# A squared-ReLU MLP in split fp32: the first product by Strassen's seven products, the second as a phase of its own

## The chip, the cores and the metric

The kernel runs on one core of a Trainium2 chip. The metric is the device time of one launch, in microseconds. The core has a matrix engine (TensorE, PE in the profile, with its weight loads shown as PEld), a vector engine (VectorE, DVE), an activation engine (ScalarE, ACT), a general engine (GpSimd, POOL), and a queue engine (SyncE, SP), which here issues every load and store. SBUF is the on-chip memory, PSUM the eight banks of 128 x 512 fp32 into which TensorE accumulates, DRAM the memory outside.

## What is computed

One inference step of a diffusion backbone with one layer, on 128 context tokens and 2048 latent tokens: 17 tiles of 128 tokens. Tile 0 is the context, with modulation vectors of its own; tiles 1 to 16 are latent. The model width D is 1024, the MLP's inner width DFF 4096.

```python
def block(x, s0, mod, ...):
    sh1, sc1, ga1, sh2, sc2, ga2 = mod
    h = rmsnorm(x, norm_mix_l) * (1.0 + sc1) + sh1
    o, s_new = mixer(h, s0, ...)     # projections, chunked DeltaNet scans, spatial gating, output projection
    x = x + ga1 * o
    h = rmsnorm(x, norm_ffn_l) * (1.0 + sc2) + sh2
    x = x + ga2 * (jnp.square(jax.nn.relu(h @ w_ff1_l)) @ w_ff2_l)
    return x, s_new
```

A last rmsnorm (`norm_final`) follows for both streams. The change is in the MLP line alone: `h @ w_ff1` is 2176 x 1024 by 1024 x 4096, and the second product 2176 x 4096 by 4096 x 1024.

## The kernel before

**Split products.** Every large product is taken on operands split in two: `H` is the value rounded to the type fp32r (an ACT copy), `L` the rest (a DVE subtraction), each of the same size as the value. `mm3` (L205 to L210) issues three matmuls for each pair: H by H, H by L, L by H. In a matmul the first operand (128 x 128) is loaded into the array, the second streams past it, up to 512 columns at a time. `load_split` (L176 to L185) loads a 128 x 512 block of weights from DRAM and splits it.

**Order of the work.** The program is written as lists of small steps that are merged (`interleave`, and a list of events with due times for the scan phase, whose bounds stand in `WINDOWS`). A planner with a simulated timeline then fixes each engine's order. Every engine works in its own fixed order and waits on semaphores for what it needs; loads and stores go in order through SP.

**Phases.** Modulation vectors (`mod_steps`: w_mod in blocks of 128 x 512, multiplied on DVE, added up on PE), input projection and convolution, forward scan over the tiles, backward scan. In the backward scan (events from `NT` on) each tile also gets its gates and the output projection (`o_steps`; matmuls named pj, with operands oH and oL), which writes the residual to `x2_d` in DRAM. `h2_steps` then takes a tile of `x2_d`, normalises it, transposes it in eight 128 x 128 pieces on PE, applies scale and shift on ACT, and stores the MLP's input, transposed, to `h2_d`: per tile two loads and two stores of 256 KB. The tiles go from 16 down to 0; `h2_steps` runs inside the scan phase for tiles 16 to 13 (`GROUPS[0]`) and inside the MLP for the 13 others.

**The MLP** (L1311 to L1492) handles four groups of tiles: (16..13), (12..9), (8..5) and (4..0). For each group it goes through eight blocks of 512 columns of DFF. `wload` brings 8 blocks of w_ff1 and 8 of w_ff2 of 256 KB (L183, L184 split them); the pools `wp` (48 buffers) and `stage` that hold them are the same as in the phases before. `ff1` makes 4 products of 128 columns of DFF by the group's tokens: 8 x 3 matmuls of 512 columns into one bank (named f), or, for the last group with its 640 tokens, 2 x 8 x 3 of 320 columns. Then ReLU on ACT (L1443), the square on DVE (L1444), and the split into zH (L1445, ACT) and zL (L1446, DVE), which stay in SBUF. The second product (`part`, matmuls named yps or pm) takes for each tile and each half of D the four blocks j, 4 x 3 matmuls, into one bank, and DVE adds the bank to a sum in SBUF (L1470; ACT copies it for the first block). After a group's last block `finish` multiplies by the gate, adds `x2_d`, normalises and stores; for the last group `residual` and `close` do this with most of it ahead of the last block. The last 16 steps of `mod_steps` (jc 10 and 11) run inside the first group. `split_h` loads the next group's `h2_d` and splits it (L1334). No barrier stands between the scan phase and the MLP: both use the pools `wp`, `stage` and `pmp`.

Of the kernel before, what the change touches and what calls it, by code (L numbers as in the profile page):

```python
# [17 lines left out]
P = 128  # L18
D = 1024
# [9 lines left out]
GROUPS = [(16, 15, 14, 13), (12, 11, 10, 9), (8, 7, 6, 5), (4, 3, 2, 1, 0)]  # L29
# [23 lines left out]
NV = 7  # L53
WINDOWS = [2.46, 0.03, -0.51, 1.06, -1.61, 18.16, 17.58, 18.3,
# [4 lines left out]
def hybrid_step(  # L59
# [42 lines left out]
    x2_d = dp.tile([NTOK, D], F32, name="x2_d")  # L102

# [54 lines left out]
    pmp = ctx.enter_context(tc.tile_pool(name="pmp", bufs=1, space=PSUM))  # L158
# [10 lines left out]
    wp = ctx.enter_context(tc.tile_pool(name="wp", bufs=48))  # L169
    sp = ctx.enter_context(tc.tile_pool(name="stage", bufs=NS))  # L170
# [34 lines left out]
    def mm3(ps, trip, first=True, last=True):  # L205
        n = len(trip)
        for i, (lh, ll, rh, rl) in enumerate(trip):
            T.matmul(ps, lh, rh, start=first and i == 0, stop=False)  # L208
            T.matmul(ps, lh, rl, start=False, stop=False)  # L209
            T.matmul(ps, ll, rh, start=False, stop=last and i == n - 1)  # L210
# [6 lines left out]
    def mod_steps(jc, pool):  # L217
# [3 lines left out]
        def f(k):  # L221
            raw = raw_w(w_mod[0, k * P : (k + 1) * P, jc * 512 : (jc + 1) * 512], sp, "raw")
# [8 lines left out]
            if k == KT - 1:  # L231
                ps = pm1()
# [550 lines left out]
    def h2_steps(t, psum, tmp):  # L783
# [4 lines left out]
        def norm2():  # L788
            u["x"] = x = [w512("x"), w512("x")]
# [31 lines left out]
    with ExitStack() as ph:  # L821
# [432 lines left out]
        for i, u in enumerate(units):  # L1254
# [9 lines left out]
            if i >= NT:  # L1264
# [4 lines left out]
                if u["t"] in GROUPS[0]:  # L1269
# [39 lines left out]


    with ExitStack() as ph:  # L1311
        p4h = ph.enter_context(tc.tile_pool(name="p4h", bufs=1))
        p4 = ph.enter_context(tc.tile_pool(name="p4", bufs=1))
        psy = ph.enter_context(tc.tile_pool(name="p4y", bufs=3, space=PSUM))
        psf = ph.enter_context(tc.tile_pool(name="p4f", bufs=3, space=PSUM))

        late_mods = [st for jc in range(10, 12) for st in mod_steps(jc, p4)]
        ga2 = []
        nf = [wrow(norm_final[n * 512 : n * 512 + 512].unsqueeze(0)) for n in range(2)]

        def split_h(gi):

            tiles = GROUPS[gi]
            c0, n = tiles[-1] * P, len(tiles) * P
            hH, hL, steps = [], [], []

            def f(k, s, m):
                if s == 0:
                    hH.append(p4h.tile([P, 640], F32R, tag=f"hH{k}", name="hH4"))
                    hL.append(p4h.tile([P, 640], F32R, tag=f"hL{k}", name="hL4"))  # L1330
                raw = w512("hraw")
                load(out=raw[:, :m], in_=h2_d[:, k, c0 + s : c0 + s + m])
                A.copy(hH[k][:, s : s + m], raw[:, :m])
                V.tensor_tensor(out=hL[k][:, s : s + m], in0=raw[:, :m], in1=f32(hH[k])[:, s : s + m],  # L1334
                                op=ALU.subtract)

            for k in range(KT):
                for s, m in segments(n):
                    steps.append(lambda k=k, s=s, m=m: f(k, s, m))
            return hH, hL, steps  # L1340

        def segments(n):
            return [(0, 512)] if n == 512 else [(0, 320), (320, 320)]

        def wload(b, steps=[]):
            w1 = []
            for k in range(KT):
                w1.append(load_split(w_ff1[0, k * P : (k + 1) * P, b * 512 : (b + 1) * 512]))
                for st in steps[k : k + 1]:
                    st()  # L1350
            w2 = [[load_split(w_ff2[0, (b * 4 + j) * P : (b * 4 + j + 1) * P, m * 512 : (m + 1) * 512])
                   for j in range(4)] for m in range(2)]
            return w1, w2

        NB = DFF // 512
        ny = []
        finishing = []
        nxt = split_h(0)
        for gi, tiles in enumerate(GROUPS):
            if gi == 1:  # L1360
                ga2 += [wrow(mod_d[1:2, 5 * D + n * 512 : 5 * D + n * 512 + 512]) for n in range(2)]
            nt = len(tiles)
            segs = segments(nt * P)
            hH, hL, _ = nxt
            y = [p4.tile([P, D], F32, tag=f"y{i}", name="y4") for i in range(nt)]
            pos = {t: (t - tiles[-1]) * P for t in tiles}

            def finish(i, t, y=y):
                yt = y[i]
                for n in range(2):  # L1370
                    ga = ga2[n]
                    if cond(t) == 0:
                        ga = wrow(mod_d[0:1, 5 * D + n * 512 : 5 * D + n * 512 + 512])
                    sl = slice(n * 512, (n + 1) * 512)
                    x = w512("x4")
                    load(out=x, in_=x2_d[t * P : (t + 1) * P, sl])
                    V.tensor_tensor(out=yt[:, sl], in0=yt[:, sl], in1=ga, op=ALU.mult)
                    V.tensor_tensor(out=yt[:, sl], in0=yt[:, sl], in1=x, op=ALU.add)
                ss = smp.tile([P, 1], F32, tag="ss", name="ss")
                r = smp.tile([P, 1], F32, tag="r", name="r")  # L1380
                junk = p4.tile([P, D], BF16, tag="junk", name="junk")
                A.activation(junk, yt, AF.Square, accum_out=ss)
                rsqrt_cols(r, ss, 1, 1.0 / D, EPS)
                for n in range(2):
                    sl = slice(n * 512, (n + 1) * 512)
                    V.scalar_tensor_tensor(out=yt[:, sl], in0=yt[:, sl], scalar=r, in1=nf[n], op0=ALU.mult,
                                           op1=ALU.mult)
                store(out=yrow(t), in_=yt)

            gates, sums, outs = {}, {}, {}  # L1390

            def residual(i, t, y=y, gates=gates):

                for n in range(2):
                    ga = ga2[n]
                    if cond(t) == 0:
                        ga = wrow(mod_d[0:1, 5 * D + n * 512 : 5 * D + n * 512 + 512])
                    sl = slice(n * 512, (n + 1) * 512)
                    x = w512("x4")
                    load(out=x, in_=x2_d[t * P : (t + 1) * P, sl])  # L1400
                    V.tensor_tensor(out=y[i][:, sl], in0=y[i][:, sl], in1=ga, op=ALU.mult)
# [135 lines left out]
```

## Time and profile before

| | us |
|---|---|
| median of 3 runs | 2792.97 |
| lowest, highest | 2790.7, 2798.1 |
| the profiled execution | 2793.13 |
| its span, from first to last activity | 2791.4 |

The profile is one execution recorded by the hardware. Busy time is the time in which an engine had an instruction at work. A row of the timeline gives the start, the length, the engine, the line of the program, the operation, what it writes and reads, the shape, and how many records it joins; in brackets what the engine waited for. Matmuls are pipelined: the length of one is its latency, and the distance between two starts is what it costs. A row of a table of groups gives the line, engine, operation, names, shape and count, then the busy time and the mean length in ns, then the idle time before them and what ended it. A row of stretches gives start and end, length, and for PE, PEld, DVE, ACT and POOL the busy time and number of records, then the clock granted to TensorE as a share of full speed, the busy share of the DMA engines, and GB/s. A plain fp32 matmul appears as two records, a split (fp32r) one as one.

### The profile page before, as it was taken

Reading aid. Unit: us, or ns where it says so; the run is one execution under the profiler, and the core shown is the slowest. Engines: PE = TensorE matmul, PEld = TensorE weight load, DVE = VectorE, ACT = ScalarE, POOL = GpSimd, SP = SyncE. Lnnn points to the kernel's source line nnn. Section 1 sums busy time; section 2 is a strip of 40 time slices with the busy share of each in tenths; the row PEclk is TensorE's granted clock in tenths of the full one; section 3 lists DMA queues with packets and bytes.
Section 4 is the critical chain, followed back from the end, with each engine's and each line's share of the span. In section 5 each row is a group of like instructions: output and inputs, shape, how many; then the busy total and the mean of one; then the engine's idle time right before and its main releaser. Section 6 shows DMA issues by size and latency. Waiting matters only on the chain.

```text
span 2791.4 us, 45476 instructions
## 1 busy us (share of the span) xinstructions
PE 2742.4 (98%) x16466; PEld 2326.1 (83%) x16466; DVE 1722.4 (62%) x3688; ACT 1284.3 (46%) x3137; POOL 225.9 (8%) x448
## 2 busy tenths in 40 slices
PE   8999998999999899999999999999999999999998
PEld 5999997888887777888878888888888888899988
DVE  5867656777777887865556574454744556444456
ACT  4655555555555566544334343343433434422332
POOL 3121113111111111100000000000000000000000
PEclk9999998999999999999999999999999999999999
DMA  8866648555455666535244443344433454322232
GB/s 292 270 199 209 197 140 279 169 162 160 153 165 184 210 215 220 182 123 161 87 136 151 140 155 99 110 133 133 152 107 96 131 153 141 120 71 61 72 95 83
DMA packets 339910, 426.74 MB, mean 153 GB/s; under 512 B 27404, under 2 KB 187580, under 8 KB 339686
## 3 DMA queue, kind: packets, MB, share of 16 engines
q1 hardware_dynamic: 339686, 423.85, 48.5%
q8 instruction: 129, 2.11, 0.3%
q14 instruction: 95, 0.78, 0.1%
HBM read 338.38 MB, written 85.37 MB: 152 GB/s over the span
## 4 chain that ended last, share of the span: by engine, by line
PE 86%; DMA 7%; DVE 4%; ACT 1%; issue 1%; SPq 1%; POOL 0%; POOLq 0%; ACTq 0%; DVEq 0%
PE f L208 8%; PE f L209 8%; PE f L210 8%; PE yps L210 7%; PE yps L208 7%; PE yps L209 7%; PE pj L208 6%; PE pj L210 6%; PE pj L209 6%; PE pm L208 3%; PE pm L210 3%; PE pm L209 3%; PE pd L867 3%; DMA raw<-in_w_ff_dram 2%; DMA qT<-qT_d 1%; DMA raw<-in_w_mod_dram 1%
## 5 line engine op out<-in xcount | busy, mean ns | idle before, releaser
L184 DVE TENSOR_TENSOR wL<-raw,wH 128x512 fp32r<-128x512 f32 x584 | 393.3, 690 | 200.4 <-ACT wH L183 192.8
L183 ACT CAST wH<-raw 128x512 fp32r<-128x512 f32 x584 | 354.6, 622 | 334.1 <-DMA raw<-in_w_ff_dram 269.9
L208 PE MATMUL f<-hH,wH 128*128 128x512 f32 (+1 forms) x1280 | 457.1, 358 | 1.8 <-ACT rl L1443 1.8
L209 PE MATMUL f<-hL,wH 128*128 128x512 f32 (+1 forms) x1280 | 454.7, 357 | 0.0
L210 PE MATMUL f<-hH,wL 128*128 128x512 f32 (+1 forms) x1280 | 451.7, 357 | 0.0
L208 PE MATMUL yps<-wH,zH 128*128 128x512 f32 x816 | 318.9, 391 | 0.0
L209 PE MATMUL yps<-wL,zH 128*128 128x512 f32 x816 | 317.7, 389 | 0.0
L210 PE MATMUL yps<-wH,zL 128*128 128x512 f32 x816 | 313.7, 389 | 0.0
L208 PEld LDWEIGHTS f<-hH,wH 128*128 128x128 f32 x1280 | 240.2, 188 | 33.8 <-ACT rl L1443 3.6
L209 PEld LDWEIGHTS f<-hL,wH 128*128 128x128 f32 x1280 | 240.3, 188 | 30.1
L210 PEld LDWEIGHTS f<-hH,wL 128*128 128x128 f32 x1280 | 240.2, 188 | 30.0
L1444 DVE TENSOR_TENSOR sq<-rl 128x512 f32<-128x512 f32 (+1 forms) x160 | 96.4, 609 | 263.8 <-ACT rl L1443 263.8
L1443 ACT ACTIVATE rl<-f 128x512 f32<-128x512 f32 (+1 forms) x160 | 83.7, 532 | 318.1 <-PE f L210 318.1
L208 PE MATMUL pj<-kH,wH 128*128 128x386 f32 (+2 forms) x568 | 190.5, 338 | 0.3 <-DVE kH L450 0.3
L210 PE MATMUL pj<-kH,wL 128*128 128x386 f32 (+2 forms) x568 | 190.3, 335 | 0.0
L209 PE MATMUL pj<-kL,wH 128*128 128x386 f32 (+2 forms) x568 | 189.5, 334 | 0.0
L1470 DVE TENSOR_TENSOR y<-y,yps 128x512 f32<-128x512 f32 x171 | 114.0, 683 | 109.2 <-PE yps L210 109.1
L208 PEld LDWEIGHTS yps<-wH,zH 128*128 128x128 f32 x816 | 153.2, 188 | 32.9 <-issue 0.9
L210 PEld LDWEIGHTS yps<-wH,zL 128*128 128x128 f32 x816 | 153.1, 188 | 32.8 <-issue 0.9
L209 PEld LDWEIGHTS yps<-wL,zH 128*128 128x128 f32 x816 | 153.2, 188 | 31.1
L167 POOL TENSOR_TENSOR r<-rsq,nhalf 128x1 f32<-128x1 f32 (+1 forms) x38 | 22.3, 588 | 1589.4 <-DVE rsq L166 1589.4
L1446 DVE TENSOR_TENSOR zL<-sq,zH 128x512 fp32r<-128x512 f32 (+1 forms) x160 | 96.5, 611 | 68.6 <-ACT zH L1445 67.4
(354 smaller groups left out, 5583.9 us busy)
## 6 DMA issues: line engine op xcount, KB each, us to landing
raw<-in_w_ff_dram SPq DMA_DIRECT2D x512, 256.0 KB
raw<-in_w_mod_dram SPq DMA_DIRECT2D x96, 256.0 KB
x<-x_d SPq DMA_DIRECT2D x68, 256.0 KB
raw<-in_w_in_dram SPq DMA_DIRECT2D x48, 256.0 KB
hH<-hH_d SPq DMA_DIRECT2D x42, 256.0 KB
hL<-hL_d SPq DMA_DIRECT2D x42, 256.0 KB
gb<-g_d SPq DMA_DIRECT2D x34, 256.0 KB
KK<-kk_d SPq DMA_DIRECT2D x34, 256.0 KB
```

The costliest lines, as they stand in the source:

```text
L167: G.tensor_tensor(out=out, in0=t[:np_, :n], in1=nhalf[:np_, :n], op=ALU.pow)
L183: A.copy(h, raw)
L184: V.tensor_tensor(out=lo, in0=raw, in1=f32(h), op=ALU.subtract)
L208: T.matmul(ps, lh, rh, start=first and i == 0, stop=False)
L209: T.matmul(ps, lh, rl, start=False, stop=False)
L210: T.matmul(ps, ll, rh, start=False, stop=last and i == n - 1)
L867: T.matmul(p[:, h, :], lhs[:, h, :], rhs[:, h, :], start=True, stop=True)
L1443: A.activation(rl[:, :m], ps[:, :m], AF.Relu)
L1444: V.tensor_tensor(out=sq[:, :m], in0=rl[:, :m], in1=rl[:, :m], op=ALU.mult)
L1446: V.tensor_tensor(out=zl[:, s : s + m], in0=sq[:, :m], in1=f32(zh)[:, s : s + m], op=ALU.subtract)
L1470: V.tensor_tensor(out=ys, in0=ys, in1=ps, op=ALU.add)
```

## The change

- **First product by Strassen's method.** The pools `wp`, `stage` and `pmp` are closed (`wst.close()`) after the scan phase, and new pools are opened. 2048 latent tokens are taken in two groups of 1024 (tiles 9 to 16, then 1 to 8). Tokens (two halves of 512), D (two halves of 512) and pairs of 128 columns of DFF form a 2 x 2 by 2 x 2 block product. In the form used (Winograd's), seven products of sums of blocks take the place of eight. `token_steps` makes the token operands of a group once: 28 loads of 256 KB from `h2_d`, 16 DVE sums, 28 splits (copy on ACT, subtraction on DVE), kept in seven buffers `hop`. `weight_steps` makes the weight operands of one unit (256 columns of DFF): two loads of 512 KB, four sums, seven splits (eight in the second group). `unit` takes the seven products, each 4 x 3 matmuls of 512 columns, partly on top of one another in PSUM (`onto`), adds the rest on DVE, applies ReLU and square, and stores four blocks of 256 KB to a new DRAM buffer `z_d`. There are 2 x 16 units; the weights of a unit are prepared among the steps of the unit before it.
- **Tile 0** doesn't fit the block form. `single` computes it in the second group: 48 matmuls of 128 columns for each unit.
- **h2.** `h2_steps` now runs in the scan phase for tiles 16 to 9; the nine others run two steps at a time inside the first units.
- **The second product is a phase of its own,** with new pools. Tiles go in six groups, (14..16), (11..13), (8..10), (5..7), (2..4), (0, 1). For each group all 32 blocks j of DFF are added up in PSUM (`part`), two banks a tile. For each pair of blocks `operands` loads w_ff2 (two loads of 512 KB) and z (one load) and splits them. w_ff2 is thus read six times instead of four, and z is written to DRAM and read back. `finish` reads the banks directly. The steps of `mod_steps` for jc 10 and 11 move into the first group of this phase.
- The launch also sets a size for a DMA scratch area (`dynamic_dma_scratch_size=1024`).

```diff
+    z_d = dp.tile([P, DFF // P, NTOK], F32, name="z_d")
...
-                if u["t"] in GROUPS[0]:
+                if u["t"] > 8:
                     spread(i + p3[8], i + p3[9], h2_steps(u["t"], pj, fraw), "fill")
...
+    wst.close()
...
+        def token_steps(c0):
+            ops, b, tt = {}, {}, {}
+            def raw(n, kp):
+                kh, th = divmod(n, 2)
+                r = t512("hraw")
+                load(out=r, in_=h2_d[:, kh * 4 + kp, c0 + th * 512 : c0 + th * 512 + 512])
+                return r
+            def put(i, kp, src):
+                if kp == 0:
+                    ops[i] = fh.tile([P, 4, 2, 512], F32R, tag="hop", name="hop", bufs=7)
+                A.copy(ops[i][:, kp, 0, :], src)
+                V.tensor_tensor(out=ops[i][:, kp, 1, :], in0=src, in1=f32(ops[i])[:, kp, 0, :], op=ALU.subtract)
+            def p1(kp):
+                put(1, kp, raw(0, kp))
+            def p5(kp):
+                x, y = raw(1, kp), raw(0, kp)
+                V.tensor_tensor(out=x, in0=x, in1=y, op=ALU.subtract)
+                tt[kp] = x
+                put(5, kp, x)
...
+            return ops, [lambda f=f, kp=kp: f(kp) for f in (p1, p5, p6, p7, p2) for kp in range(4)]
...
+        def weight_steps(jp, extra):
...
+                    load(out=t, in_=w_ff1[0, kh * 512 : kh * 512 + 512, jp * 256 : jp * 256 + 256]
+                         .rearrange("(a p) c -> p a c", p=P))
...
+        def unit(jp, c0, w, ops):
+            def product(i, onto=None):
+                if onto is None:
+                    ps[i] = bank()
+                p = ps[i if onto is None else onto]
+                h, lo = w[i]
+                mm3(p, [(h[:, kp, :], lo[:, kp, :], ops[i][:, kp, 0, :], ops[i][:, kp, 1, :]) for kp in range(4)],
+                    first=onto is None, more=onto is not None)
...
+            def s7():
+                product(7)
+                p7 = t512("p7")
+                A.copy(p7, ps[7])
+                V.tensor_tensor(out=p7, in0=p7, in1=u["x"], op=ALU.add)
+                V.tensor_tensor(out=p7, in0=p7, in1=u["p5"], op=ALU.add)
+                rl2(p7, p7)
+                out(1, 1, p7)
...
+            return [s1, s5, s6, s7, s3, s2, s4]
+
+        def single(jp, w, x):
+            ps = bank()
+            for i, (a, b) in enumerate(((1, 2), (0, 4))):
+                mm3(ps[:, i * P : i * P + P],
+                    [(w[n][0][:, kp, :], w[n][1][:, kp, :], x[0][:, kh * 4 + kp, :], x[1][:, kh * 4 + kp, :])
+                     for kh, n in enumerate((a, b)) for kp in range(4)])
...
+        later = [st for t in range(8, -1, -1) for st in h2_steps(t, bank, t512, t512)]
+        ops, steps = token_steps(9 * P)
+        w, prep = weight_steps(0, False)
+        interleave(steps, prep)
+        for n, (gi, jp) in enumerate(todo):
+            main = unit(jp, c0, w, ops)
+            if gi == 1:
+                main.append(lambda jp=jp, w=w: single(jp, w, x0))
+            nw, prep = weight_steps(todo[n + 1][1], todo[n + 1][0] == 1) if n + 1 < len(todo) else (None, [])
+            extra = later[:2]
+            del later[:2]
...
+            interleave(*[x for x in (main, prep, extra) if x])
+            if n == NP - 1:
+                ops, steps = token_steps(P)
+                for st in steps:
                     st()
...
+        def weights(j):
+            raw = gw.tile([P, D], F32, tag="raw", name="raw", bufs=3)
+            load(out=raw, in_=w_ff2[0, j * P : (j + 1) * P, :])
...
+        def tokens(j, t0, n):
+            raw = gw.tile([P, 2, 384], F32, tag="zraw", name="zraw", bufs=3)
+            load(out=raw[:, :, :n], in_=z_d[:, j : j + 2, t0 * P : t0 * P + n])
...
+        def finish(t, ps):
...
+            for n in range(2):
+                sl = slice(n * 512, n * 512 + 512)
+                V.tensor_tensor(out=y[:, sl], in0=ps[n], in1=gates[c][:, sl], op=ALU.mult)
+            for n in range(2):
+                sl = slice(n * 512, n * 512 + 512)
+                V.tensor_tensor(out=y[:, sl], in0=y[:, sl], in1=x[:, sl], op=ALU.add)
+                A.activation(x[:, sl], y[:, sl], AF.Square, accum_out=ss[:, n : n + 1])
...
+        groups = [(14, 3), (11, 3), (8, 3), (5, 3), (2, 3), (0, 2)]
+        for g, (t0, nt) in enumerate(groups):
+            ps = [[None, None] for _ in range(nt)]
+            def part(i, j, od, ps=ps):
+                (wh, wl), (zh, zl) = od
+                if j == 0:
+                    ps[i] = [bank(), bank()]
+                c = slice(i * P, i * P + P)
                 for n in range(2):
+                    m = slice(n * 512, n * 512 + 512)
+                    mm3(ps[i][n], [(zh[:, c], zl[:, c], wh[:, m], wl[:, m])], first=j == 0, last=j == NJ - 1)
+            od = {}
+            for j in range(0, NJ, 2):
+                nxt = operands(g, j)
+                od[j], od[j + 1] = nxt
+                if j < GL:
+                    continue
...
+                if g == 0:
+                    for st in mods[:2]:
+                        st()
+                    del mods[:2]
+            for i in range(nt):
+                finish(t0 + i, ps[i])
```

More of the change, by code (lines that the diff above doesn't have):

```diff
@@ L1317, in hybrid_step @@
[L1317 to L1340, printed above, removed]
@@ new lines, in hybrid_step, with first_tile @@
+        x0 = []
+        def first_tile():
+            raw = [t512("x0"), t512("x0")]
+            x0.extend(fh.tile([P, KT, P], F32R, tag=f"x0{i}", name="x0", bufs=1) for i in range(2))
+            for i, r in enumerate(raw):
+                s = slice(i * 4, i * 4 + 4)
+                r3 = r.rearrange("p (k t) -> p k t", k=4)
+                load(out=r3, in_=h2_d[:, s, 0:P])
+                A.copy(x0[0][:, s, :], r3)
+                V.tensor_tensor(out=x0[1][:, s, :], in0=r3, in1=f32(x0[0])[:, s, :], op=ALU.subtract)
```

328 lines of the change are left out of this document (177 added, 151 removed).

## The prediction

> **What bounds the kernel now.** I read first the busy shares and the chain that ended last, then the busy time by stretches, then single rows for the price of each operation.
>
> ```profile
> span 2791.4 us, 45476 instructions
> PE 2742.4 (98%) x16466; PEld 2326.1 (83%) x16466; DVE 1722.4 (62%) x3688; ACT 1284.3 (46%) x3137; POOL 225.9 (8%) x448
> PE 86%; DMA 7%; DVE 4%; ACT 1%; issue 1%; SPq 1%; POOL 0%; POOLq 0%; ACTq 0%; DVEq 0%
> ```
>
> TensorE is busy 98% of the span and carries 86% of the chain. The stretches around the MLP (length, then busy time of PE, its loads, DVE, ACT, POOL, then granted clock, DMA share, GB/s):
>
> ```profile
> 0.00:70.00 70.00, 62.08 (x263) 35.81 (x264) 36.66 (x122) 31.19 (x63) 21.79 (x104) 1.00 0.86 292
> 1265.00:1291.00 26.00, 26.00 (x118) 21.51 (x117) 18.51 (x31) 12.33 (x21) 0.00 (x0) 1.00 0.65 206
> 1291.00:2783.70 1492.70, 1490.88 (x7151) 1267.77 (x7149) 789.13 (x1302) 570.87 (x1082) 17.37 (x29) 1.00 0.37 116
> 2783.70:2791.40 7.70, 0.00 (x0) 0.00 (x0) 2.99 (x7) 1.90 (x5) 0.55 (x1) 0.68 0.36 136
> ```
>
> From 1291 to 2783.7 us PE is idle for 1.8 us in all, DVE half the time: the MLP lasts as long as its matmuls. Between 1265 and 1291 PE never stops either, though the phase changes there:
>
> ```profile
> 1264.77 0.49 PE L1195 MATMUL pm<-ident,ob 128*128 128x128 f32 x3
> 1265.01 0.47 PE L208 MATMUL f<-hH,wH 128*128 128x512 f32 x1
> 1281.01 0.39 PE L210 MATMUL pj<-wH,oL 128*128 128x512 f32 x1
> ```
>
> The first MLP product (f) starts 16 us before the last output projection (pj): MLP work fills the waits of the mixer's end. The change ends that overlap.
>
> **Prices.** A matmul's duration is its latency; what it costs is the distance to the next.
>
> ```profile
> 2499.78 0.39 PE L208 MATMUL pm<-wH,zH 128*128 128x512 f32 x1
> ...
> 2501.14 0.39 PE L208 MATMUL yps<-wH,zH 128*128 128x512 f32 x1
> 2699.70 0.31 PE L209 MATMUL f<-hL,wH 128*128 128x320 f32 x1
> ...
> 2700.88 0.39 PE L208 MATMUL yps<-wH,zH 128*128 128x512 f32 x1
> 1279.65 0.68 DVE L1218 TENSOR_TENSOR tmp<-pj,row 128x512 f32<-128x512 f32 x1
> ...
> 1282.08 0.69 DVE L1334 TENSOR_TENSOR hL<-hraw,hH 128x512 fp32r<-128x512 f32 x1
> ```
>
> Six intervals in 1.36 us: 0.2267 us for 512 columns. Eight in 1.18 us: 0.1475 for 320. Four DVE operations of 512 columns in 2.43 us: 0.606 each.
>
> ```profile
> L208 PE MATMUL f<-hH,wH 128*128 128x512 f32 x768 | 299.0, 390 | 1.8 <-ACT rl L1443 1.8
> L208 PE MATMUL f<-hH,wH 128*128 128x320 f32 x512 | 158.2, 309 | 0.0
> ```
>
> There are three such lines, so before the first product takes 2304 matmuls of 512 columns and 1536 of 320.
>
> **Step 1, seven products for eight.** For sixteen tiles, each unit (1024 tokens by 256 of DFF) takes 7 x 4 x 3 = 84 matmuls of 512 columns, against 96. Over 32 units 384 go: 384 x 0.2267 = **-87.1**. The sums are DVE's: some 20 operations a unit (22 in the second token group), 13 us against 19.0 us of PE, and weights are made a unit ahead, so steady units stay PE's and the added DVE work costs nothing; without that cover each DVE operation would cost 0.6 us x 32.
>
> **Step 2, tile 0 alone.** Tile 0 rode in the last group of five: 1536 x 0.1475 = 226.6 for five tiles, of which four would take 768 x 0.2267 = 174.1, so it cost 52.5 us. Now it takes 768 matmuls of 128 columns, each with a weight load of its own. No split product of 128 columns stands in the trace. The nearest rows:
>
> ```profile
> 428.09 0.28 PE L208 MATMUL pj<-kH,wH 128*128 128x258 f32 x1
> 428.21 0.28 PE L209 MATMUL pj<-kL,wH 128*128 128x258 f32 x1
> 428.46 0.53 PEld L631 LDWEIGHTS pt<-scr,mcum 128*128 128x128 f32 x4
> L208 PEld LDWEIGHTS f<-hH,wH 128*128 128x128 f32 x1280 | 240.2, 188 | 33.8 <-ACT rl L1443 3.6
> 1247.49 1.05 PE L867 MATMUL pd<-vt,T 128*128 128x128 f32 x8
> L867 PE MATMUL pd<-vt,T 128*128 128x128 f32 x272 | 39.7, 281 | 0.0
> 21.22 0.57 PEld L350 LDWEIGHTS pt<-ident,xh 10*128 10x128 f32 x8 [0.86 <-issue]
> L350 PEld LDWEIGHTS pt<-ident,xh 10*128 10x128 f32 x8 | 0.6, 137 | 0.9 <-issue 0.9
> ```
>
> The narrowest split products, of 258 columns, start 0.12 us apart. At L631, a plain fp32 product, only 68 columns move, and four loads lie (0.53 - 0.19)/3 = 0.114 us apart; the loads of the split products last the same 0.19. At L867 a plain fp32 product of 128 columns is two records of (1.05 - 0.28)/7 = 0.11, 0.22 in all. At L350 loads of ten rows come each (0.57 - 0.14)/7 = 0.061. The columns themselves, by the two prices above, need 0.1475 - 192 x (0.2267 - 0.1475)/192 = 0.068. So the price lies between 0.068 and 0.222; I take 0.114, from the row where a full load of the same 0.19 us sets the pace: 768 x 0.114 = 87.6, **+35.1** (ends 0 and +118).
>
> For this the Trainium skill, "TensorE: Matmul & The Clock Gate", section "LDWEIGHTS (loading the stationary operand)", gives a load as its columns over 1.2 per ns, 107 ns here; L631 agrees within 7 ns, and by the page tile 0 would be an estimated 82 us instead of 87.6.
>
> **Step 3, start of the first product's phase.** The weight and staging pools are closed first, and the new ones take their memory, so the first load of h2 waits for the last projection and the last stores. Nothing is fetched ahead, and the f products that filled the waits until 1281 now come later. What is late next is DVE: in its order 74 operations stand before the last operand of unit 0 (28 splits and 16 sums of tokens, 15 splits and 10 sums of weights, 5 others): 74 x 0.606 = 45 us. Bytes are not later: 28 x 256 KB and 6 x 512 KB are 10.5 MB, 36 us at the 292 GB/s of the first 70 us (should the w_ff1 loads, whose rows of 1 KB are half those of before, run at half that rate, which no row shows, 46 us, still no later than DVE). Before them the first transfer lands:
>
> ```profile
> 1.23 3.74 SPq L174 DMA_DIRECT2D raw<-in_w_mod_dram  x8
> 4.40 8.80 PE L298 MATMUL pm<-raw,scond 128*2 128x512 f32 x16 [4.40 <-DMA raw<-in_w_mod_dram]
> ```
>
> about 3 us from issue to use. PE meanwhile does the seven products as operands come, 19 us; the last product (2.7 us) comes after DVE. With 1.5 for the first copy and split, 3 + 1.5 + 45 + 2.7 - 19 = 33. The last 48 products pj fill 11.2 of the 16.2 us to 1281.2; f products filled the other 5, of which I put some 4 down as waits that now stand open:
>
> ```profile
> 1265.00:1300.00 35.00, 11.20 (x48) 9.01 (x48) 2.04 (x3) 0.00 (x0) 1.00 0.55 174
> ```
>
> **+37** (30 to 46).
>
> **Step 4, change of token group.** The second group's 44 splits and sums, and the weights of the next units, stand behind unit 15's outputs on DVE: 87 operations to the end of unit 17's weights, 53 us, against 2 x (19.0 + 48 x 0.114) = 49 us of PE work in units 16 and 17, whose last product follows the last operand: 53 + 2.7 + 1 - 49 = **+8** (5 to 20).
>
> **Step 5, start of the second product's phase.** Again all memory changes hands: z of the last unit must be stored before z is read. Six weight blocks (3.1 MB), z for them and the next (1.6), tile rows of x2, gates, the final norm and the first modulation blocks that the queue takes in ahead (3.3) are 8 MB, 28 us at 292 GB/s; PE spends 18 x 0.2267 = 4.1 us on each block, and goes through them one by one, so it has four done when the sixth lands: 3 + 28 - 4 x 4.1 = 14.6, **+14** (9 to 25). z is written and read, 35.6 MB each way, and w_ff2 read six times for four; with both phases near 100 to 240 GB/s that is hidden elsewhere. The matmuls of this product stay 3264 of 512.
>
> **Step 6, ends.** Sums stay in PSUM: 272 additions and copies out of it go from DVE and ACT, which PE did not wait for: 0. At five changes of group PE waits for banks that `finish` still reads: **+6** (0 to 12). The last two tiles end together, behind some eleven DVE operations after the last matmul, instead of
>
> ```profile
> 2783.26 0.39 PE L210 MATMUL pm<-wH,zL 128*128 128x512 f32 x1
> 2788.10 0.38 SPq L1423 DMA_DIRECT2D out_dram<-tmp  x1
> ```
>
> 7.75 us to the span's end: eleven operations 6.7, the root and scaling some 1.6, and 3.3 from the last store's issue to the end, as here: 11.6, **+3.9**. h2 of tiles 9 to 12 moves into the scans: each tile two loads and two stores on SP's queue, two ACT squares and eight ACT evictions, eight transposes on PE:
>
> ```profile
> 1249.87 0.60 PE L1195 MATMUL pm<-ident,ob 128*128 128x128 f32 x4
> 900.00:1265.00 365.00, 352.65 (x3002) 288.73 (x3000) 282.04 (x738) 204.60 (x645) 49.69 (x59) 0.99 0.60 189
> ```
>
> 0.11 each, 0.88 a tile, 3.5 us more where PE is busy 97% and 3.5 us fewer in the MLP: 0; the queue has room there (189 GB/s).
>
> **Sum:** -87.1 + 35.1 + 37 + 8 + 14 + 6 + 3.9 = +16.9, a span of 2808.3 us. The profiled run took 2793.13 for a span of 2791.4, 1.7 more, and lies 0.2 above the median of 2792.97: 2810.0.
>
> **Rivals.** *Narrow products at the fp32 price.* If 128 columns fall to the two passes of L867, 0.222 (or cost as much as 512 columns, 0.2267), tile 0 takes 170 to 174 us, 83 to 87 more: 2893 to 2897. For it: no split product narrower than 258 columns stands in the rows, and the loads last exactly as those of fp32. Against it: each split product is one record, not two.
>
> *The loads hide, and the kernel is faster.* If the loads of narrow products follow one another as at L350, the columns set the pace, 0.068 to 0.08 a product; tile 0 costs 52 to 61 and the sum falls by 26 to 35: 2775 to 2784. It decides below 0.08. Against it: L631, where little moved and a full load still set the pace; at L350 ten rows are loaded. The Trainium skill, the same page, section "Back-to-back issue gap", gives about 81 ns for streams of 128 columns: 62 us for tile 0, an estimate of 2785; the same sentence has 131 ns at 512 columns, where this trace shows 226.7.
>
> *Longer hand-overs.* If the phase starts take their upper ends (46, 20, 25 instead of 37, 8, 14), 32 more: 2842. For it: both starts have a cold queue and two engines in series; against it: PE gets partial work all along.
>
> *The change doesn't deliver, units wait for DVE.* In the first group 20 operations would have to outlast 19.0 us, 0.95 us each; here they take 0.606, with DVE at half load. At 1.07 sixteen units lose 2.4 each: 2848. The second group, with tile 0's products on PE, would need 1.1.
>
> **How the numbers follow.** 0.3% of 2793 is 8.4 us, about what a measurement of this kernel can tell from no change: the bounds are 2784.6 and 2801.4. Likeliest, 0.114 with hand-overs within their ranges: 0.46, own range 2795 to 2832, a quarter of it within 0.3%. Narrow products at the fp32 price: 0.26. Loads that hide: 0.14, of which 0.10 faster (with hand-overs no shorter than forecast at 0.08 it comes to no change). Longer hand-overs: 0.11. DVE-bound units: 0.03. Faster 0.10; same 0.12 + 0.04 = 0.16; slower 0.74. The range leaves out the lower part of hidden loads and what exceeds the fp32 price: 2786 to 2897.
>
> **What would show it.** Step 1: 2688 matmuls of 512 columns in the first product, 0.2267 apart, about 19.0 us from unit to unit. Step 2: distance between 128-column matmuls, 0.114; the whole forecast hangs on it, 10 ns is 7.7 us. Step 3: PE idle about 37 us after the last pj, chain on DVE's splits. Step 4: idle around unit 16. Step 5: idle at the first yps, ended by DMA. Step 6: about 11.6 us after the last matmul. Wrong would be a narrow product off 0.114, DVE waits in every unit, or phase starts under 30 us in all.

## The result and the profile after

The changed kernel takes 2811.62 us (median of four runs, 2808.85 to 2817.55) against 2791.97 for the kernel before: a ratio of 1.0069, 95% interval 1.0047 to 1.0091. The forecast was 2810. The profiled execution took 2810.78 us, its span 2809.1, 17.7 longer than before. The busy shares and the chain that ended last, of the changed kernel:

```profile
span 2809.1 us, 44803 instructions
PE 2716.0 (97%) x16082; PEld 2269.6 (81%) x16082; DVE 1817.0 (65%) x3625; ACT 1293.6 (46%) x2980; POOL 230.4 (8%) x448
PE 83%; DVE 7%; DMA 7%; ACT 1%; issue 1%; SPq 1%; POOL 0%; DVEq 0%; POOLq 0%; ACTq 0%
```

TensorE has 384 records fewer, and DVE's share of the chain went from 4% to 7%. Where that is, the stretches show (start and end, length, busy time of PE, its loads, DVE, ACT, POOL, granted clock, DMA share, GB/s):

```profile
1286.90:1296.20 9.30, 0.19 (x1) 0.02 (x1) 2.13 (x4) 1.24 (x2) 0.00 (x0) 0.75 0.54 173
1296.20:1342.40 46.20, 32.57 (x88) 19.56 (x89) 45.24 (x78) 26.68 (x49) 2.14 (x1) 0.75 0.67 227
1637.90:1663.00 25.10, 16.17 (x62) 11.01 (x61) 20.58 (x33) 13.16 (x23) 0.00 (x0) 0.86 0.85 306
1663.00:2043.40 380.40, 380.40 (x2054) 328.47 (x2052) 227.01 (x353) 115.67 (x205) 0.00 (x0) 1.00 0.27 90
2043.40:2060.00 16.60, 7.33 (x26) 5.89 (x26) 8.34 (x11) 6.46 (x8) 0.00 (x0) 0.69 0.78 284
2060.00:2798.40 738.40, 738.40 (x3249) 608.20 (x3247) 390.20 (x436) 284.37 (x342) 10.04 (x15) 1.00 0.64 210
2798.40:2809.10 10.70, 0.15 (x1) 0.00 (x0) 6.40 (x14) 2.78 (x8) 1.10 (x2) 0.75 0.26 98
```

PE stands at three places: the start of the first product (from 1287), the change of token group (from 1638) and the start of the second product (from 2043). In the first DVE is busy 45.24 of 46.20 us, in the second the transfers run at 306 GB/s. Between them, and through all 738 us of the second product, PE never waits. The timeline rows at these places (the rows between them are left out):

```profile
1286.70 0.39 PE L216 MATMUL pj<-wH,oL 128*128 128x512 f32 x1
1342.40 0.48 PE L214 MATMUL f<-hop,wH 128*128 128x512 f32 x1
1637.71 0.39 PE L216 MATMUL f<-hop,wL 128*128 128x512 f32 x1
1644.12 0.79 PE L214 MATMUL f<-hop,wH 128*128 128x512 f32 x1 [6.02 <-ACT hop L1358]
1817.86 0.22 PE L214 MATMUL f<-x,wH 128*128 128x128 f32 x1
1823.06 0.28 PE L216 MATMUL f<-x,wL 128*128 128x128 f32 x1
2043.20 0.28 PE L216 MATMUL f<-x,wL 128*128 128x128 f32 x1
2052.74 2.93 PE L214 MATMUL yps<-wH,zH 128*128 128x512 f32 x6 [9.27 <-ACT wH L1572]
2798.16 0.39 PE L216 MATMUL yps<-wH,zL 128*128 128x512 f32 x1
```

1342.40 is the first matmul of unit 1, so from the last projection to the end of unit 0 pass 55.7 us for 19.0 us of products. The two rows of f<-x are the first and the last of one unit's 48 narrow products: (1823.06 - 1817.86)/47 = 0.1106 us each. In what follows "lost" is the sum of the distances between starts of matmuls beyond their price (0.2267 for 512 columns, 0.1106 for tile 0's and for a transpose): 36.0 us at the first place, 14.2 at the second, 11.2 at the third, some 0.5 in the rest of the second product.

Not all of it is waiting. Behind each of the three waits the first products lie 0.43 us apart in place of 0.2267, and the granted clock there is 0.50. At the third place PE loses 9.4 us before its first product and 1.8 with the products behind it:

```profile
2052.70:2056.10 3.40, 3.36 (x8) 2.69 (x9) 3.29 (x3) 2.67 (x3) 0.00 (x0) 0.50 1.03 386
```

### The profile page after: what moved, and what is told of

Read it like the earlier page. It is cut to its first block, busy times and chain, and to the rows that moved or that the text cites. A ratio compares the mean times of both kernels' runs of the same rounds, so it can differ in the third digit from the quotient of the medians.

```text
span 2809.1 us, 44803 instructions
## 1 busy us (share of the span) xinstructions
PE 2716.0 (97%) x16082; PEld 2269.6 (81%) x16082; DVE 1817.0 (65%) x3625; ACT 1293.6 (46%) x2980; POOL 230.4 (8%) x448
## 3 DMA queue, kind: packets, MB, share of 16 engines
q1 hardware_dynamic: 378502, 501.45, 55.7%
## 4 chain that ended last, share of the span: by engine, by line
PE 83%; DVE 7%; DMA 7%; ACT 1%; issue 1%; SPq 1%; POOL 0%; DVEq 0%; POOLq 0%; ACTq 0%
PE yps L214 9%; PE yps L215 9%; PE yps L216 9%; PE f L215 8%; PE f L216 8%; PE f L214 8%; PE pj L214 6%; PE pj L216 6%; PE pj L215 6%; PE pd L874 2%; DMA qT<-qT_d 1%; DMA QK<-qk_d 1%; PE pm L214 1%; PE pm L215 1%; PE pm L216 1%
## 5 line engine op out<-in xcount | busy, mean ns | idle before, releaser
L214 PE MATMUL yps<-wH,zH 128*128 128x512 f32 x1088 | 415.0, 391 | 9.3 <-ACT wH L1572 9.3
L215 PE MATMUL yps<-wL,zH 128*128 128x512 f32 x1088 | 423.5, 389 | 0.0
L216 PE MATMUL yps<-wH,zL 128*128 128x512 f32 x1088 | 423.2, 389 | 0.0
L214 PE MATMUL f<-hop,wH 128*128 128x512 f32 x896 | 356.5, 399 | 18.6 <-ACT wH L1341 9.1
L215 PE MATMUL f<-hop,wH 128*128 128x512 f32 x896 | 355.7, 397 | 11.7 <-DVE hop L1359 11.6
L1573 DVE TENSOR_TENSOR wL<-raw,wH 128x1024 fp32r<-128x1024 f32 x192 | 234.5, 1224 | 195.1 <-ACT wH L1572 194.3
L216 PE MATMUL f<-hop,wL 128*128 128x512 f32 x896 | 353.8, 395 | 0.0
L1572 ACT CAST wH<-raw 128x1024 fp32r<-128x1024 f32 x192 | 201.1, 1051 | 255.9 <-PE yps L216 153.4
L214 PEld LDWEIGHTS f<-hop,wH 128*128 128x128 f32 x896 | 171.3, 191 | 57.5 <-ACT hop L1358 11.2
L215 PEld LDWEIGHTS f<-hop,wH 128*128 128x128 f32 x896 | 170.7, 191 | 55.0 <-DVE hop L1359 21.3
L216 PEld LDWEIGHTS f<-hop,wL 128*128 128x128 f32 x896 | 170.8, 191 | 35.3 <-DVE wL L1342 0.2
L1341 ACT CAST wH<-raw 128x512 fp32r<-128x512 f32 x112 | 69.5, 620 | 155.4 <-PE f L215 149.8
```

The lines of the kernel that those rows point to most:

```text
L214: T.matmul(ps, lh, rh, start=first and i == 0, stop=False, skip_group_check=more)
L215: T.matmul(ps, lh, rl, start=False, stop=False, skip_group_check=more)
L216: T.matmul(ps, ll, rh, start=False, stop=last and i == n - 1, skip_group_check=more)
L1341: A.copy(h, src)
L1572: A.copy(h, raw)
L1573: V.tensor_tensor(out=lo, in0=raw, in1=f32(h), op=ALU.subtract)
```

## The experiments

Times are medians; each group of kernels was compared with runs of the kernel before on the same chip, 2792.39 (first four), 2794.34 (next four), 2792.43 (three) and 2790.69 (last). These differ by up to 4 us, so a difference between kernels of two groups is no better than that.

### h2 of four tiles in the scan, alone

```diff
 (the kernel before)
-                if u["t"] in GROUPS[0]:
+                if u["t"] > 8:
...
-                if gi + 1 < len(GROUPS) and 1 <= b <= len(GROUPS[gi + 1]):
+                if 0 < gi and gi + 1 < len(GROUPS) and 1 <= b <= len(GROUPS[gi + 1]):
```

> The kernel before, with one part of the change alone: h2 of tiles 12 to 9 is made in the backward scan instead of in the MLP's first group. Theory A (what the two traces suggest: the scan falls 13 us behind over these four tiles): the scan phase ends 9 to 13 us later, the MLP's first group gets 3.5 us shorter, so about +6 to +10 us, 2798 to 2802. Rival B (my forecast: 3.5 us move from one place to another): 2792, within 2 us. Rival C (the planner makes room by other means, as it orders the whole program anew): faster than 2790.

Measured: 2799.11, +6.7 us; ratio 1.0021 (1.0011 to 1.0030). Theory A holds, rival B falls. The last step of the scan's chain, in the timelines of the kernel before, of the changed kernel and of this one:

```profile
1240.77 0.94 PE L867 MATMUL pd<-S,kT 128*128 128x128 f32 x7
```
```profile
1251.68 0.94 PE L874 MATMUL pd<-S,kT 128*128 128x128 f32 x7
```
```profile
1253.73 0.94 PE L867 MATMUL pd<-S,kT 128*128 128x128 f32 x7
```

Eleven to thirteen us later for 3.5 us of transposes; in the traces of all the kernels below that keep these h2 steps in the scan, it is 6 to 13 us later. The waits of PE between 1080 and 1190 us in the changed kernel name one part; the kernel before has none there:

```profile
PE pd L960 <- DVE P L951: 3.9, 8, 1.2
```

The scan is a chain between PE and DVE, and among its steps now stand the h2 steps with their own trip over ACT, DVE and POOL. The 3.9 us are a part; what makes the rest of the delay no run here shows.

### Eight plain products for seven

```diff
-            return ops, [lambda f=f, kp=kp: f(kp) for f in (p1, p5, p6, p7, p2) for kp in range(4)]
+            return ops, [lambda n=n, kp=kp: put(n, kp, raw(n, kp)) for n in (0, 2, 1, 3) for kp in range(4)]
...
-            return w, [first, fifth, sixth, seventh, third, second, fourth]
+            return w, [lambda x=x: whole(*x) for x in ((1, 0, 0), (2, 0, 1), (0, 1, 0), (4, 1, 1))]
...
-            return [s1, s5, s6, s7, s3, s2, s4]
+            return [lambda i=i, th=th, kh=kh: half(i, th, kh) for th in range(2) for i in range(2) for kh in range(2)]
```

`half` takes 12 matmuls of one block of D, and after the second block applies ReLU and square and stores. Token loads and splits fall from 28 to 16 a group, and the `hop` buffers from seven to four.

> The changed kernel with eight plain products for seven: four token blocks and four weight blocks are split, no sums, 96 matmuls a unit; phases, stores and the second product stay. Theory (the seven products save their 384 matmuls in full, and the operands' preparation is paid at the two starts of a token group): +87.1 for the matmuls, the start of the phase 16 to 20 us shorter, the change of group 6 to 8 shorter: 2870 to 2878. Rival (the preparation costs nothing beside the fixed hand-over): 2897 to 2900. Rival (Strassen's units lose part of the saving to waits): below 2865.

Measured: 2871.14, 59.5 more than the changed kernel, about as expected. Lost at the start of the phase: 20.2 us in place of 36.0; at the change of group 7.8 in place of 14.2. So of the 87.1 us that seven products save, 15.8 + 6.4 = 22 are paid back for the preparation of their operands (loads, sums and splits), at the two places where PE has nothing else to do; 65 remain by the profile, 59.5 by the medians.

### Tile 0 with 64 columns

```diff
-                mm3(ps[:, i * P : i * P + P],
-                    [(..., x[0][:, kh * 4 + kp, :], x[1][:, kh * 4 + kp, :])
+                mm3(ps[:, i * 64 : i * 64 + 64],
+                    [(..., x[0][:, kh * 4 + kp, 0:64], x[1][:, kh * 4 + kp, 0:64])
```

> The changed kernel with the first product of tile 0 over 64 of its 128 tokens, copied to the other 64 (so the context output is wrong): 768 matmuls of 64 columns for 128. Theory (the weight load sets the pace): the distance between these matmuls stays at 0.11 us and the time within 2 us of 2811. Rival (columns set the pace, 0.0004 us each by the prices of 512 and 320): 0.084 us, 20 us less, 2791.

Measured: 2845.01, 33 us *more*. Both were wrong on the time; the rows tell why. Timeline of this kernel, one unit's narrow products, and the stretch of the second token group:

```profile
1985.34 0.28 PE L215 MATMUL f<-x,wH 128*128 128x64 f32 x1
...
1987.80 0.28 PE L216 MATMUL f<-x,wL 128*128 128x64 f32 x1
...
1988.77 0.40 PE L216 MATMUL f<-x,wL 128*128 128x64 f32 x1
...
1991.97 0.40 PE L216 MATMUL f<-x,wL 128*128 128x64 f32 x1
```
```profile
1663.00:2070.00 407.00, 407.00 (x1997) 350.62 (x1995) 223.23 (x348) 117.58 (x248) 0.00 (x0) 0.91 0.25 82
```

The first pair lies 22 steps apart: 0.112 us each, as with 128 columns, so the columns don't set the pace. That fits the weight load, which the rivals left as the only named cause; a fixed cost of another kind was not told apart from it. The second lies 15 steps apart: 0.213, about double. The granted clock fell to half for some 72 us of this stretch, in eleven pieces (mean 0.91, where the changed kernel has 1.00), and the 512-column products under it lay 0.43 us apart: half of 72 us is 36, about what the kernel lost. PE was busy without a break all the while. With half the columns the array streams for a smaller part of the time; that this is what lowered the clock was not shown. With 128 columns it stayed at 1.00.

### The token sums left out

```diff
-                V.tensor_tensor(out=x, in0=x, in1=y, op=ALU.subtract)
                 tt[kp] = x
... (likewise in p6, p7 and p2)
```

> The changed kernel without the 16 DVE sums of token blocks in each group (the splits and loads stay, the MLP's output is wrong). Theory: the start of the phase is DVE's, so it gets 16 x 0.606 = 9.7 us shorter; the change of token group is set by its 28 loads (DMA share 0.85 at 306 GB/s there), so it stays: 2800 to 2803. Rival (my forecast, DVE in both places): 19 us less, 2792. Rival (transfers in both): no change, 2811.

Measured: 2805.1, 6.5 less by the medians; the profiled spans differ by 10.1, of which 4.6 lie ahead of the MLP, in the scan phase, which the edit leaves alone. Lost at the start: 27.5 for 36.0, 8.5 less (9.7 expected), so DVE's operations set that place. Lost at the change of group: 17.5 for 14.2, more with 16 operations fewer on DVE. PE's first wait there stayed (6.4 us, for ACT's copy of a block that had not landed; 6.0 in the changed kernel), and a second of 2.8 us came to it. So DVE's sums don't set this place, and the rival with DVE in both places falls.

### Tile 0 turned round

```diff
-            for i, (a, b) in enumerate(((1, 2), (0, 4))):
-                mm3(ps[:, i * P : i * P + P], [... (w, x) with 128 columns of x ...])
+            mm3(ps[:, 0:256], [(x[0][:, kh * 4 + kp, :], x[1][:, kh * 4 + kp, :], w["kh", kh][0][:, kp, :],
+                                w["kh", kh][1][:, kp, :]) for kh in range(2) for kp in range(4)])
...
+                T.transpose(ps[:, i * P : i * P + P], y[:, i * P : i * P + P], ident)
```

The splits of w_ff1 that tile 0 needs are made 256 columns wide, in six buffers of their own; of those of 128 columns ten are left of 18.

> The changed kernel with tile 0's first product turned round: the 128 tokens are the loaded operand, 256 columns of weights stream, 24 matmuls and two transposes a unit in place of 48 matmuls of 128 columns. Theory (tile 0 pays for weight loads, 0.11 us each, whatever streams under 0.11): 24 x 0.121 + 0.22 = 3.1 us a unit in place of 5.3, 34 us less in all, 2775 to 2780. Rival (split products of 256 columns and fewer have a price of their own, as in the rival of the prediction): 24 x 0.22 + 0.22 = 5.5, no gain, 2812 to 2816. Rival (the transposes make PE wait for ACT and DVE): between, with PE idle in each unit.

Measured: 2780.37, 31 less than the changed kernel; against the kernel before 0.9955 (0.9939 to 0.9971). First and last product of one unit in its timeline:

```profile
1831.25 0.28 PE L214 MATMUL f<-wH,x 128*128 128x256 f32 x1
...
1834.00 0.28 PE L216 MATMUL f<-wH,x 128*128 128x256 f32 x1
```

2.75 us over 23 steps: 0.120 each for 256 columns, against 0.1106 for 128. Half as many products cost half as much, as the theory has it. It would have been 35 us, but the change of group now lost 21.9 us in place of 14.2; why was not tested on this kernel.

### The second group's tokens early

```diff
+            if n == NP - 1:
+                nops, st = token_steps(P)
+                s1, s5, s6, s7, s3, s2, s4 = main
+                main = [s1] + st[0:4] + [s5] + st[4:8] + [s6] + st[8:12] + [s7, s3] + st[12:16] + [s2, s4] + st[16:20]
             interleave(*[x for x in (main, prep, extra) if x])
             if n == NP - 1:
-                ops, steps = token_steps(P)
-                for st in steps:
-                    st()
+                ops = nops
```

> The changed kernel with the second group's token operands made among unit 15's products, each behind the product that frees its buffer, so that their 28 loads start some 19 us earlier. Theory (the change of group waits for the loads): the 14 us at units 15 and 16 fall to 2 to 5, 2799 to 2803. Rival (DVE is the bound there: its operations only move ahead of unit 15's outputs): less than 4 us gained.

Measured: 2798.37, 13 less. Units 15 and 16 in its stretches:

```profile
1637.00:1683.00 46.00, 45.20 (x241) 38.57 (x240) 43.66 (x74) 23.33 (x42) 0.00 (x0) 1.00 0.53 163
```

1.4 us are lost in place of 14.2. DVE and the queue have the same work, but start it while PE still has unit 15 to do. The first token loads of the second group, in the changed kernel and in this one:

```profile
1637.60 3.41 SPq L1352 DMA_DIRECT2D hraw<-h_d  x6
```
```profile
1622.69 14.63 SPq L1352 DMA_DIRECT2D hraw<-h_d  x17
```

In the changed kernel they are issued when PE is at the last product of unit 15 (1637.71), here 15 us sooner.

### Two units at once at the start

```diff
+        both = [unit(jp, 9 * P, x, ops) for jp, x in ((0, w), (1, w1))]
+        for s, st in enumerate((steps[0:4], steps[4:8], steps[8:12], steps[12:16], [], steps[16:20], [])):
+            interleave(*[x for x in (st, [prep[s], prep1[s]]) if x])
...
+            both[0][s]()
+            both[1][s]()
```

> The changed kernel with units 0 and 1 taken product by product together (eight banks), h2 steps three at a time from unit 2 on. Theory (the start of the phase is DVE's chain of token operands; PE has only one unit's work to do beside it): DVE has some 78 operations, 47 us, PE 38 us of work beside them, and both units are done 12 us earlier: 2798 to 2802. Rival (the start is set by the hand-over of memory and by transfers): less than 3 us gained. Rival (the second unit's weights push DVE's chain out by their full 11 operations): 5 to 7 us gained.

Measured: 2810.43, 1.2 less: a miss. Lost from the last projection to the end of unit 2: 39.9 us, against 37.8 for the same place in the changed kernel. The raw blocks of w_ff1 have four buffers here in place of three. The stretch, the waits of PE in it, and those of SP's queue:

```profile
1293.50:1376.00 82.50, 64.59 (x234) 48.72 (x235) 68.63 (x114) 38.03 (x69) 0.56 (x1) 0.85 0.55 177
```

```profile
PE f L214 <- ACT hop L1358: 13.0, 4, 5.1
PE f L214 <- ACT wH L1341: 9.3, 1, 9.3
```
```profile
SPq L1396 <- DVE s L1416: 9.4, 1, 9.4
SPq L1352 <- DVE hraw L1372: 8.8, 4, 7.6
```

The 9.3 us are the wait for the phase's first product, which the changed kernel has too (9.1). Waits for ACT's copies of token blocks (hop) grew to 13.0 us from 2.0 over the same units of the changed kernel, while those for DVE's splits of them fell from 9.2 to 2.5: here the blocks come late, no longer DVE. SP issues loads in order, and each waits for a buffer: a load of weights (L1396) for one that DVE still reads, and the token blocks (L1352) behind it. With two units under way the buffers run out, and DVE is no busier (68.63 of 82.5 us) than over the same units of the changed kernel (72.98 of 87.40). What PE gained in work it lost in waits. More work for PE was not enough here, where the token blocks kept their twelve buffers; that more of them would have brought the 12 us was not tried.

### h2 behind the scan

```diff
+                    t = u["t"]
+                    lo, hi = (i + p3[8], i + p3[9]) if t > 12 else (2 * NT + H2A + (12 - t) * H2B, 2 * NT + H2A + (13 - t) * H2B)
+                    spread(lo, hi, h2_steps(t, pj, fraw), "fill")
```

> The changed kernel with h2 of tiles 12 to 9 planned behind the last scan step, beside the last output projections, instead of beside the scans. Theory (these steps cost more than their matmuls because they stand in the way of the scan's chain): 6 to 9 us less, 2803 to 2806. Rival (their cost is the same anywhere, or they now delay the first loads of the next phase): within 3 us of 2812, or more.

Measured: 2819.61, 8 us more: the rival. The scan's last step is back at 1241.08 us:

```profile
1241.08 0.94 PE L876 MATMUL pd<-S,kT 128*128 128x128 f32 x7
```

so the scan loses nothing, but from the last projection, now at 1291.3, to the end of unit 0 pass 62.0 us in place of 55.7: the token loads of the next phase wait for h2's stores (4.2 us the longest), and all but the first few come behind the last of them.

### Both gains, and two attempts on top

The first of these takes tile 0 turned round, now at the head of each unit, and the early tokens together; the second moves h2 to one step before the scan's end (H2A = -1.0, H2B = 0.35); the third replaces `V.tensor_tensor` by `G.tensor_tensor` in the 16 token sums.

> The changed kernel with tile 0's product turned round and the second group's tokens made early, both as before, and tile 0's product placed first in each unit instead of last. If the two gains (31 and 13 us) are at different places they add up: 2765 to 2768, and a little less because unit 16 has tile 0's matmuls to do while its operands come: 2761 to 2768. Rival (the two share a stall, or the turned product now waits at the head of the unit): 2772 or more.

> As e9_both, with h2 of tiles 12 to 9 planned from one step before the last scan step on, 20 us earlier than in e8_late. Theory (in e8_late the scan lost nothing, 13 us less than in the changed kernel, and the loss came back because the last h2 store stood before the first loads of the next phase): now neither, 6 to 9 us less than e9_both. Rival (PE has no free time there, and the steps hold up the last projections): equal or slower than e9_both.

> As e9_both, with the 16 sums of token blocks in each group on POOL in place of DVE. Leaving them out altogether shortened the first unit by 8.3 us. Theory (DVE's own work sets the start): 4 to 8 us less than e9_both, if a sum takes POOL about 1 us. Rival (POOL and DVE slow each other, or POOL's chain takes over: 16 sums of 2 us or more): equal or slower.

Measured: 2774.98, 2788.69 and 2783.68. The gains did not add up: the first lost 15.8 us at the change of group, where the early tokens alone lost 1.4. Its longest wait of PE there:

```profile
PE f L214 <- ACT x L1463: 10.4, 1, 10.4
```

ACT's copy of a finished bank stood in order behind copies of token blocks that had not landed. Moving h2 (second) went to the rival: the scan lost nothing, but PE, in order, waited at the transposes between the last projections:

```profile
PE pj L815 <- DVE x L808: 11.9, 3, 5.7
```

So h2 of these four tiles was tried at three places, with 3.5 us of matmuls each time: in the scans it cost 6.7 us, measured alone; behind them 8 us more than in them; at their end 13.7 more. POOL's sums (third) also went to the rival. First unit of the third kernel: DVE's splits, POOL's sums; then DVE's splits in the first unit of the first kernel:

```profile
L1360 DVE TENSOR_TENSOR hop<-hraw,hop 128x512 fp32r<-128x512 f32 x27 | 24.8, 954 | 1.8 <-ACT hop L1359 1.8
...
L1367 POOL TENSOR_TENSOR hraw<-hraw 128x512 f32<-128x512 f32 x4 | 7.0, 1787 | 32.5 <-DMA hraw<-h_d 32.5
```
```profile
L1359 DVE TENSOR_TENSOR hop<-hraw,hop 128x512 fp32r<-128x512 f32 x27 | 17.9, 694 | 0.0
```

A sum takes POOL 1.8 us. The 0.95 us of a DVE split is a mean of two kinds: 19 of the 27 took 0.68, much as without POOL (0.69), and eight, each beside a sum on POOL, 1.10 to 1.78. One of these and its sum:

```profile
1310.58 1.75 DVE L1360 TENSOR_TENSOR hop<-hraw,hop 128x512 fp32r<-128x512 f32 x1
```
```profile
1310.07 1.72 POOL L1373 TENSOR_TENSOR hraw<-hraw 128x512 f32<-128x512 f32 x1
```

The split ends some 0.5 us after the sum, as if it had waited for it. The first unit got 7.4 us longer (53.1 for 45.7).

### Two small buffers

```diff
-            z = t512("z0")
+            z = fw.tile([P, 256], F32, tag="zz", name="z0", bufs=2)
...
-            z = t512("z1")
+            z = fw.tile([P, 256], F32, tag="zz", name="z1", bufs=2)
```

> As e9_both, with tile 0's z in two small buffers of its own in place of two of the twelve 128 x 512 buffers that the loads of token blocks also take. In e9_both units 15 and 16 took 59.8 us for 41.2 us of matmuls, with PE waiting 10.4 us for a copy that stood on ACT behind splits whose loads came late; in e6_early the same place lost 1.3 us. Theory (the loads came late because the buffers were held): the wait goes, 10 to 17 us less than e9_both, 2758 to 2765. Rival (the head of the unit is the wrong place for tile 0's product, buffers or not): within 4 us of e9_both.

Measured: 2760.4, 14.6 less than without, and against the kernel before 0.9885 (0.9867 to 0.9904): the fastest of all, 30 us under the kernel before. At the change of group PE is busy throughout:

```profile
1620.00:1664.00 44.00, 44.00 (x219) 37.33 (x218) 41.74 (x66) 25.82 (x44) 0.00 (x0) 1.00 0.78 252
```

So it was the buffers: two of twelve, held by tile 0's z, delayed the loads, these ACT's copies, and these PE. At the change of group 0.1 us are lost in place of 15.8. The starts of the two phases stay (37.3 and 12.4 us lost).

## Why the prediction was right, and where it was not

The measured time lies 1.6 us from the forecast, but several terms of the sum were off and cancelled.

- **Step 1** (-87.1): right. 2688 products at 0.2267, and from 1663 on PE never waits in a unit.
- **Step 2** (+35.1): the price was 0.1106 against 0.114, so 84.9 us and +32.4. That the columns don't set the pace was shown by the 64 columns; that it is the load fits, by the row of L631. The fp32 rival (0.222) and the rival that loads hide (below 0.08) both fall. The Trainium skill's rule for a weight load ("TensorE: Matmul & The Clock Gate", "LDWEIGHTS (loading the stationary operand)": 107 ns) agrees within 4 ns; its 81 ns for streams of 128 columns (section "Back-to-back issue gap") does not hold for these operands.
- **Step 3** (+37, of which 33 behind the last projection): 36.0 lost there, 9.3 before the first product (the forecast has 3 + 1.5) and 26.7 after it (45 + 2.7 - 19 = 28.7). The mechanism, DVE's chain of splits and sums, was shown by leaving out the sums (8.5 us of the 9.7 that 16 x 0.606 makes); the hand-over ahead of it was set too short.
- **Step 4** (+8): 14.2. Size and cause were off. The forecast counted 87 operations of DVE; without 16 of its sums the place lost 17.5. PE's longest wait is for a token block whose load is issued only at the end of unit 15, and some 3 us are products at half clock behind that wait. With loads, copies and splits begun 15 us earlier, 1.4 are lost.
- **Step 5** (+14): 11.2. The place and its start were right, the course was not: the forecast had 3 us before the first block and the rest as waits until the sixth had landed. PE lost 9.4 us before the first product, none for later blocks, and 1.8 at half clock, of which the forecast says nothing. That 11.2 lies near 14 is luck in part.
- **Step 6**: the change of groups of the second product cost 0 in place of +6, the end 10.9 - 8.1 = +2.8 in place of +3.9 (from the start of the last matmul to the end of the span, less the same before). *The four h2 tiles, which I costed at nothing beyond 3.5 us moved, are the step that failed*: the kernel before with this part alone is 6.7 us slower. In the changed kernel the last projection starts 5.7 us later though some 5 us of f products no longer stand before it; less the 3.5 that is 7.2, where step 3 had 4 for waits left open. This is one trace: in ten traces of kernels with this scan phase the last projection starts between 1282.1 and 1289.1 us, so the 7.2 is good to some 4.

Measured: -87.1 + 32.4 + 36.0 + 7.2 + 14.2 + 11.2 + 0 + 2.8 = 16.7, of 17.7 us by which the spans differ. The forecast had 16.9: 12.4 too little at steps 3 and 4 and for h2, 12.6 too much at steps 2, 5 and 6. That these met is luck. What decides the sign held: tile 0's narrow products and three starts without other work cost more than 384 matmuls save. No hand-over reached the upper end that the rival of longer hand-overs gave it (46, 20, 25), and units in mid-group never waited for DVE.

## What to carry to other kernels

A method that saves matmuls is worth its saving less what its operands cost where nothing else runs: here 22 of 87 us, plus the hand-overs of two phases that were one before. What stands apart from the block form (one tile of seventeen) can eat half of the rest; put the narrow side where it is loaded, not where it streams. Before moving a step into a phase whose engine is full, price its trip over all engines, not its matmuls, and count the buffers that everything in flight holds.

## What the runs showed of the hardware

- Split products of 64 and 128 columns cost the same, 0.11 us, at full clock; 256 cost 0.120, 320 cost 0.1475, 512 cost 0.2267.
- Behind a wait of 9 us the granted clock was 0.50 and the first products of 512 columns lay 0.43 us apart, 1.8 us more in all at the start of the second product.
- The granted clock also fell to half, for some 72 of 407 us, in a stream in which PE never stood, when a fifth of a unit's time went to 64-column products; with 128 columns it stayed at 1.00. The Trainium skill ("TensorE: Matmul & The Clock Gate", "HAM oscillation — how this bites in real kernels") tells of this for idle gaps; here there were none.
- While POOL summed 128 x 512 fp32 blocks, DVE's subtractions of such blocks that ran into a sum took up to 1.78 us in place of 0.68. The Trainium skill ("SBUF — State Buffer", "Who interferes with whom") says that a DVE instruction with two SBUF inputs contends with a GpSimd instruction that reads SBUF; the runs agree.
